# A hybrid decoder layer in one kernel: transposes ahead of the data, first loads on two queues, another bank order, the compressing preparation pinned, one multiplication moved

## The chip, the cores and the metric

The kernel runs on one core of a Trainium2 chip. The metric is the device time of one execution in microseconds (us); lower is better. TensorE (PE) multiplies, VectorE (DVE) and ScalarE (ACT) do elementwise work, GpSimd (POOL) does some elementwise work and issues stores, SyncE (SP) issues loads.

## The reference

For x of 1024 tokens by 1024 channels, in float32, one layer:

```
xn   = rmsnorm(x, norm1_w);  proj = xn @ w_in      # q, k/v of 3 branches, gates, xr, yr, 2 merge gates
A    = sparse attention(q, compressed k/v, selected blocks, window of 512), weighted by gates
B    = RG-LRU(causal conv of width 4 of xr) * gelu(yr)
x    = x + (sigmoid(g_a) * (A @ W_a_up) + sigmoid(g_b) * (B @ W_b_up)) @ W_o
out  = x + relu(rmsnorm(x) @ W1)^2 @ W2
```

The compressed keys and values are a two-layer network over blocks of 32 tokens: blocks plus a learned position, times a 2048x256 matrix, gelu, times 256x64.

## The kernel before

**Precision.** Every product of two float32 matrices is three products of 32-bit round operands: each operand is split into a high part (ACT copies it to the type fp32r) and a low part (DVE subtracts), and high*high, high*low and low*high are summed in PSUM. So each tile that TensorE takes costs ACT and DVE one operation each. For weights this is `split_w` (L197 to L202: `wh` by L200 on ACT, `wl` by L201 on DVE), with four buffers of 512 columns for each part, which is two streamed weight tiles.

**Order on the engines.** The program is written in one order, and a planner in the build gives each engine a fixed list of instructions: of those that are ready in its plan, the one that stands first in the program. An engine runs its list in order. `tc.issue_after(ins)` puts the instructions of its block that are on the engine of `ins` behind `ins` in that list.

**Stage 1, the start.** SP issues the loads: `sm` (small vectors, with the norm's scale), then for each block k of 128 channels x (`xs`, the first in two halves) and 350 columns of the attention weights (`as`). POOL builds the identity. For each k, ACT and DVE split x (`xh`, `xl`) and the weights (`ah`, `al`), and TensorE adds three products for each of six token tiles to `acc6`, six banks of PSUM: five of tag "F" and one of tag "H". Two more token tiles follow in "F" banks, and then two further thirds of the columns. Tag "H" is used again by the compressing network, tag "T" (2 banks) by transposes.

**Stage 2, eight rounds j = 0 to 7 of the RG-LRU, some 26 us each (one is longer).** The work of a round in program order: TensorE computes `fx` (xr, two halves of 512 tokens, L744 to L748), with the four gate products `pg` of round j-1 between the halves; DVE takes each half out of PSUM (L748); the convolution and its split on DVE and ACT (L666 to L676; the last of it, L676, is `lst[j]["last"]`); then the pieces of the compressing network that `PHI_AT` names for this round (one in rounds 0 to 4 and 6, two in round 5: pieces 5 and 6); then `fy` (yr, two halves, out of PSUM by L767); the end of round j-1 (L712, a scan L713 on DVE, a multiplication L714 and a store L715 on POOL); then one step of `q_proc` (L555, L556, and the rope of the tile before, L423 to L425), which is queued behind L676. `fx`, `pg` and `fy` share the five "F" banks.

A piece of the compressing network is 12 products (`Hk` or `Hv`, L602) and the preparation of the next piece, `phi_prep`: four additions on DVE (L590, `zt`), the high part on ACT (L593, `zh`) and the low part on DVE (L594, `zl`).

**After that** TensorE computes the merge gates (`fg`), the attention, the two up-projections, W_o, and the two large matrices of the feed-forward part by a scheme with seven instead of eight products of halves.

Of the kernel before, what the change touches and what calls it, by code (L numbers as in the profile page):

```python
# [10 lines left out]
F32 = mybir.dt.float32  # L11
F32R = mybir.dt.float32r
AF = mybir.ActivationFunctionType
OP = mybir.AluOpType
# [3 lines left out]
P = 128  # L18
# [7 lines left out]
AW = 350  # L26
KCOFF = 4 * S
RESERVE = 2
EARLY = 8
PAD = 32  # L30
WPRI = 200
# [31 lines left out]
def stream_order():  # L63
# [13 lines left out]
    for half in range(2):  # L77
        for c in range(8):
            yield "wo", c
    for g in range(EARLY):  # L80
        yield "f1e", g
# [11 lines left out]
def product_order(n):  # L93
    out = []
    for g in range(n):
# [3 lines left out]
        out += [(g, 7), (g, 5)]  # L99
        if g + 1 < n and g + 1 >= EARLY:  # L100
            out += [(g + 1, 1), (g + 1, 2)]
# [12 lines left out]
def gap(t, off, *dims):  # L114
    return bass.AP(tensor=t.tensor, offset=t.offset + off, ap=[t.ap[0]] + [list(d) for d in dims])
# [19 lines left out]
def layer_kernel(ctx, tc, xT, w_att, w_lru, w_nsa, w_ff2, stream, rows, small, phi_w2, consts, masks, outT, scratch=None):  # L135
    nc = tc.nc
    V, A, G, T = nc.vector, nc.scalar, nc.gpsimd, nc.tensor
# [16 lines left out]
    ident = cst.tile([P, P], F32, name="ident")  # L154
    ones2 = cst.tile([P, 2], F32, name="ones2")
    sm = cst.tile([P, NSM], F32, name="sm")
# [53 lines left out]
    def ws_get(kind):  # L210
        n = st["next"]
        assert order[n][0] == kind, (n, order[n], kind)
        st["next"] += 1
        while st["prepped"] <= n:
            ws_prep()
        return st["hl"].pop(n)
# [47 lines left out]
    psT = pools.open("psT", side="left", space=PSUM)  # L264
    psA = pools.open("psA", side="left", space=PSUM)

    def attw_load(c, k):
        raw = xs_p.tile([P, AW], F32, name=f"as{k}", tag="as") if c == 0 else wa.tile([P, AW], F32, name=f"ar{c}_{k}", tag="ar", bufs=4)
        nc.sync.dma_start(raw, w_att[c, :, k])
        return raw  # L270

    def attw_split(raw, c, k):
# [9 lines left out]
    def x_load(k):  # L282
        t = xs_p.tile([P, S], F32, name=f"xs{k}", tag="xs")
        if k == 0:
            araw[(0, k)] = attw_load(0, k)
            for hs in HS:
                nc.sync.dma_start(t[:, hs], xT[0:P, hs])
        else:
            nc.sync.dma_start(t, xT[k * P:(k + 1) * P, :])
            araw[(0, k)] = attw_load(0, k)  # L290
        xs.append(t)

    nc.sync.dma_start(sm, small)
    for k in range(NK):
        x_load(k)
    make_identity(nc, ident)
    G.memset(ones2, 1.0)
    accsq = rbc
    aw = {}
    acc6 = [psA.tile([P, 512], F32, name=f"acc{t}", tag="F" if t < 5 else "H", bufs=5 if t < 5 else 1) for t in range(6)]  # L300
    for k in range(NK):
        if k == 0:
            aw[(0, k)] = attw_split(araw.pop((0, k)), 0, k)
# [59 lines left out]
    yq = [at_p.tile([P, 512], F32, name=f"yq{t}") for t in range(NT)]  # L363
# [52 lines left out]
    def rope(pool, t, nh, cosap, sinap, name):  # L416
        tmp = pool.tile([P, nh, 16], F32, name=name, tag="rp", bufs=1)
        sw = gap(t, 8, [64, nh], [-8, 2], [1, 8])
        y = gap(t, 0, [64, nh], [8, 2], [1, 8])
        t4 = gap(tmp, 0, [16, nh], [8, 2], [1, 8])  # L420
        s4 = gap(sinap, 0, [0, nh], [8, 2], [1, 8])
        c4 = gap(cosap, 0, [0, nh], [8, 2], [1, 8])
        V.tensor_tensor(t4, sw, s4, op=OP.mult)  # L423
        V.tensor_tensor(y, y, c4, op=OP.mult)
        V.tensor_tensor(y, y, t4, op=OP.add)  # L425
# [117 lines left out]
    rowq = phi_p.tile([P, 512], F32, name="rowq")  # L543
# [8 lines left out]
    def q_proc():  # L552
        for t in range(NT):
            qq = yq[t].rearrange("p (a d) -> p a d", d=64)
            V.tensor_tensor(qq, qq, gap(facq, t * 8, [1, 8], [0, 64]), op=OP.mult)  # L555
            G.tensor_tensor(yq[t], yq[t], rowq, op=OP.mult)  # L556
            yield
            rope(phi_p, yq[t], 8, qcon[:, t * 16:t * 16 + 16], qcon[:, 128 + t * 16:144 + t * 16], f"rpq{t}")

# [22 lines left out]
    def phi_prep(which, piece):  # L582
        po = SM["pos" + which][0]
        zh = phi_p.tile([P, 4, P], F32R, name=f"zh{which}{piece}", tag="zh", bufs=2)
        zl = phi_p.tile([P, 4, P], F32R, name=f"zl{which}{piece}", tag="zl", bufs=2)
        for jp in range(2):
            for g in range(2):
                src = cn_t if jp == g else cs_t
                rs = slice(jp * 64, jp * 64 + 64)
                V.tensor_tensor(gap(zt[rs], g * 64, [P, 4], [1, 63]),  # L590
                                gap(src[rs], jp + 8 * piece, [2, 4], [16, 63]),
                                gap(sm[rs], po + piece * 4, [1, 4], [0, 63]), op=OP.add)
        A.activation(zh, zt, AF.Copy)  # L593
        V.tensor_tensor(zl, zt, zh.bitcast(F32), op=OP.subtract)  # L594
        return zh, zl

    def phi_mm(H, w, zz, piece):
        zh, zl = zz
        for jj in range(4):
            h, l = w[jj // 2]  # L600
            b = slice(jj % 2 * 256, (jj % 2 + 1) * 256)
            mm3(H[:, 0:256], zh[:, jj, :], zl[:, jj, :], h[:, b], l[:, b], piece == 0 and jj == 0, piece == 3 and jj == 3)  # L602
# [59 lines left out]
    lst = {}  # L662
# [53 lines left out]

    phi = {"H": None, "zz": None}

    def phi_piece(i):
        which, piece = ("k", i) if i < 4 else ("v", i - 4)  # L720
        if piece == 0:
            phi["H"] = psB.tile([P, 512], F32, name=f"H{which}", tag="H", bufs=1)
        phi_mm(phi["H"], ws_get("phi"), phi["zz"], piece)
        ws_done()
        if i != 3 and i < 7:
            phi["zz"] = phi_prep("k" if i < 3 else "v", (i + 1) % 4)
        if piece == 3:
            bg.append(phi_tail(which, phi["H"]))

# [2 lines left out]
    for j in range(8):  # L732
        if j == 4:
            w = ws_get("vc")
            for half in range(2):
                cjob(psB, "vc", half, w, 5)
                step()
            phi["zz"] = phi_prep("v", 0)
        w = ws_get("xr")
        xy = lt("xr", j, S + P)  # L740
        xr = xy[:, 0:S + 3]
        G.memset(xr[:, 0:3], 0.0)
        for half in range(2):
            ps = ftile(psB, f"fx{j}{half}", 5)  # L744
            fjob(ps, HS[half], w)
            if half:
                ws_done()
            V.tensor_tensor(xr[:, 3 + half * 512:515 + half * 512], ps, rbc[:, HS[half]], op=OP.mult)  # L748
            if half == 0:
                step()  # L750
                if j:
                    lru_gates(j - 1)
        lru_conv(j, xr)
        lru_one(j - 1)
        lru_split(j)
        lru_root(j - 1)
        lw_prep(j)
        step()
        for i in PHI_AT[j]:
            phi_piece(i)  # L760
        w = ws_get("yr")
        y = xr[:, 3:S + 3]
        lst[j]["y"] = y
        for half in range(2):
            ps = ftile(psB, f"fy{j}{half}", 5)
            fjob(ps, HS[half], w)
            V.tensor_tensor(y[:, HS[half]], ps, rbc[:, HS[half]], op=OP.mult)  # L767
            if half:
                ws_done()
            else:  # L770
                lru_end(j - 1)
                step()
                step()
        step()
        with tc.issue_after(lst[j]["last"].ins):
            next(q_gen, None)
# [46 lines left out]
    gmps = [psC, 1]  # L823
    left[0] -= RESERVE
    mk = ab.tile([P, NMK], F32, name="mk")
# [176 lines left out]
    for ui, u in enumerate(units):  # L1002
        n = len(blocks_of(u))
        nxt = units[ui + 1] if ui + 1 < len(units) else None
        g, i, kind = u
# [7 lines left out]
        for b in range(n):  # L1013
# [18 lines left out]
            last = b == n - 1  # L1032
# [41 lines left out]

    left[0] = RESERVE + left[0]
    ins = [(rh[k], rl[k], d_lru[k * P:(k + 1) * P, :], f"rr{k}") for k in range(8)]
# [91 lines left out]
    for half in range(2):  # L1168
        hs = HS[half]
        for c in range(8):  # L1170
# [6 lines left out]
            t = vt(f"hac{c}{half}")  # L1177
# [5 lines left out]
            if c == 0:  # L1183
                acc = sq
# [4 lines left out]
            if half and c > 1:  # L1189
                norm2(c - 2, 0)  # L1190
                if c > 3:
                    k = c - 4
# [66 lines left out]
    def ff_out(g, fh, half, t):  # L1259
        A.activation(t, t, AF.Square)  # L1260
        if (fh, half) != (0, 1):
            u_store(g, {(0, 0): "B11", (1, 0): "B21", (1, 1): "B22"}[(fh, half)], t)
        if g >= EARLY or (fh, half) != (0, 0):
            uq[(g, fh, half)] = t
# [23 lines left out]
    def ff_keep(g, name):  # L1288
        t = vt(f"{name}{g}")
        ps = ff["ps"][(g, "a")]  # L1290
        if g < EARLY and name != "P1":
            V.tensor_tensor(t, ps, ff["sv"][g]["P1"], op=OP.add)
# [13 lines left out]
    def ff_product(g, p):  # L1306
        _, bn, bank = PROD[p]
        first = p in (2, 7) or p == (6 if g < EARLY else 1)
        if first:
# [4 lines left out]
        ff_done(g, p, ps)  # L1314
        if p == 3 and g < EARLY:
            t = uq[(g, 0, 0)] = vt(f"ub{g}")
# [88 lines left out]
    for g in range(EARLY):  # L1405
# [10 lines left out]
        if g < 4:  # L1416
# [4 lines left out]
            t = vt(f"T2{g}")  # L1421
# [3 lines left out]
        else:  # L1425
            name, o, half = (("T3", 0, 1), ("T1", 0, 0), ("B22", 4, 1), ("T4", 4, 0))[g - 4]
            for k in range(4):
                t = hn[(k + o, half)]
# [14 lines left out]
    for n in range(len(steps)):  # L1443
        pi, k = steps[n]
# [27 lines left out]
        elif k == 15:  # L1472
            for d in range(4):
                for kk in range(16 - DMAJ, 16):
                    mms(kk, d)
                if p in (1, 7, 6):
                    t = rs[d]
                    V.tensor_tensor(t, ps[d], t, op=OP.add)
                    kept[(p, d)] = t
                else:  # L1480
                    t = rs[d] if p == 3 else kept.pop(({4: 6, 5: 7, 2: 1}[p], d))
                    V.tensor_tensor(t, ps[d], t, op=OP.add)
                    c, half = {2: (d, 0), 3: (d, 1), 4: (d + 4, 0), 5: (d + 4, 1)}[p]
# [81 lines left out]
```

## Time and profile before

| | |
|---|---|
| median of 3 runs | 1590.0 us (1589.86 to 1592.36) |
| the profiled execution | 1590.64 us |
| its span, first to last instruction | 1588.9 us |
| TensorE matmuls busy | 1566.3 us, 99% of the span |
| VectorE busy | 1112.0 us, 70% |
| ScalarE busy | 854.5 us, 54% |
| GpSimd busy | 290.2 us, 18% |
| mean granted TensorE clock | 0.997 |

The median is 0.64 us below the profiled execution, and the profiled execution has 1.7 us outside its span. Busy time is the share in which an engine had an instruction in flight. A time in the rows below is counted from the first instruction.

### The profile page before, as it was taken

Reading aid. Unit: us, or ns where it says so; the run is one execution under the profiler, and the core shown is the slowest. Engines: PE = TensorE matmul, PEld = TensorE weight load, DVE = VectorE, ACT = ScalarE, POOL = GpSimd, SP = SyncE. Lnnn points to the kernel's source line nnn. Section 1 sums busy time; section 2 is a strip of 40 time slices with the busy share of each in tenths; the row PEclk is TensorE's granted clock in tenths of the full one; section 3 lists DMA queues with packets and bytes.
Section 4 is the critical chain, followed back from the end, with each engine's and each line's share of the span. In section 5 each row is a group of like instructions: output and inputs, shape, how many; then the busy total and the mean of one; then the engine's idle time right before and its main releaser. Section 6 shows DMA issues by size and latency. Waiting matters only on the chain.

```text
span 1588.9 us, 21949 instructions
## 1 busy us (share of the span) xinstructions
PE 1566.3 (99%) x7541; PEld 1312.3 (83%) x7541; DVE 1112.0 (70%) x2128; ACT 854.5 (54%) x1570; POOL 290.2 (18%) x414
## 2 busy tenths in 40 slices
PE   8999999999999999999999999999999999999999
PEld 8998887887888887887788888888888888888887
DVE  8637889876888777886544447988665679665664
ACT  7435667674677566675533335744555564443432
POOL 0001222233343434432000222022211110000000
PEclk9999999999999999999999999999999999999999
DMA  6101221213011121014533544355533598553554
GB/s 228 49 22 55 93 89 58 99 74 109 31 34 41 61 64 34 31 34 155 200 114 112 180 178 159 126 204 208 184 146 146 177 390 294 164 175 138 203 199 149
DMA packets 86688, 206.80 MB, mean 130 GB/s; under 512 B 11184, under 2 KB 15792, under 8 KB 86576
## 3 DMA queue, kind: packets, MB, share of 16 engines
q1 hardware_dynamic: 71856, 157.15, 28.7%
q0 software_dynamic: 14720, 48.25, 8.3%
q8 instruction: 59, 0.97, 0.2%
q14 instruction: 53, 0.43, 0.1%
HBM read 152.93 MB, written 52.43 MB: 129 GB/s over the span
## 4 chain that ended last, share of the span: by engine, by line
PE 69%; issue 2%; ACT 2%; DVE 2%; DMA 1%; POOL 1%; ACTq 0%; DVEq 0%; POOLq 0%
PE p L1462 6%; PE p L1464 6%; PE p L1463 6%; PE pt L946 3%; PE p1a L1303 3%; PE p1a L1304 3%; PE p1a L1302 3%; PE fg L234 3%; PE fg L236 3%; PE fg L238 3%; PE p1c L1304 2%; PE po L234 2%; PE po L238 2%; PE po L236 2%; PE p1c L1303 2%
## 5 line engine op out<-in xcount | busy, mean ns | idle before, releaser
L1462 PE MATMUL p<-hu,hw 128*128 128x512 f32 x448 | 174.3, 389 | 0.0
L1463 PE MATMUL p<-lu,hw 128*128 128x512 f32 x448 | 174.3, 389 | 0.0
L1464 PE MATMUL p<-hu,lw 128*128 128x512 f32 x448 | 174.3, 389 | 0.0
L201 DVE TENSOR_TENSOR wl<-wr,wh 128x512 fp32r<-128x512 f32 x156 | 110.3, 711 | 84.8 <-ACT wh L200 79.5
L200 ACT ACTIVATE wh<-wr 128x512 fp32r<-128x512 f32 x156 | 97.3, 627 | 128.7 <-PE po L236 40.7
L951 ACT ACTIVATE ph<-pt 128x512 fp32r<-128x512 f32 x148 | 88.0, 596 | 88.0 <-PE pt L946 86.7
L1139 ACT ACTIVATE hu<-ur 128x512 fp32r<-128x512 f32 x112 | 70.0, 628 | 114.4 <-PE p L1463 108.8
L952 DVE TENSOR_TENSOR pl<-pt,ph 128x512 fp32r<-128x512 f32 x148 | 101.7, 687 | 27.7 <-ACT ph L951 25.9
L234 PE MATMUL fg<-xh,wh 128*128 128x512 f32 x256 | 112.0, 437 | 5.2 <-DVE ge L792 4.8
L1140 DVE TENSOR_TENSOR lu<-ur,hu 128x512 fp32r<-128x512 f32 x112 | 77.0, 688 | 43.3 <-ACT hu L1139 37.6
L238 PE MATMUL fg<-xh,wl 128*128 128x512 f32 x256 | 101.9, 398 | 0.0
L236 PE MATMUL fg<-xl,wh 128*128 128x512 f32 x256 | 101.5, 397 | 0.0
L1464 PEld LDWEIGHTS p<-hu,lw 128*128 128x128 f32 x448 | 84.1, 188 | 17.6
L1463 PEld LDWEIGHTS p<-lu,hw 128*128 128x128 f32 x448 | 84.1, 188 | 17.5
L1462 PEld LDWEIGHTS p<-hu,hw 128*128 128x128 f32 x448 | 84.1, 188 | 17.3
L1285 ACT ACTIVATE z<-z 128x512 f32<-128x512 f32 x56 | 35.4, 632 | 53.5 <-DVE z L1284 53.4
L201 DVE TENSOR_TENSOR wlf<-S,whf 128x512 fp32r<-128x512 f32 x64 | 42.7, 689 | 27.2 <-ACT whf L200 26.5
L234 PEld LDWEIGHTS fg<-xh,wh 128*128 128x128 f32 x256 | 48.9, 191 | 14.1 <-issue 3.5
L1257 POOL DMA_DIRECT2D d_u<-z x48 | 26.0, 542 | 186.5 <-ACT z L1260 178.7
L1139 ACT ACTIVATE hw<-wr 128x512 fp32r<-128x512 f32 x64 | 39.5, 625 | 35.9 <-DVE wr L1395 17.1
L238 PEld LDWEIGHTS fg<-xh,wl 128*128 128x128 f32 x256 | 48.6, 190 | 10.8
L974 PE MATMUL o<-ph,V 128*128 128x512 f32 x132 | 54.3, 411 | 0.0
(856 smaller groups left out, 4578.1 us busy)
## 6 DMA issues: line engine op xcount, KB each, us to landing
wr<-in_stream SPq DMA_DIRECT2D x106, 512.0 KB, 3.5
ur<-d_u SPq DMA_DIRECT2D x112, 256.0 KB, 5.3
wr<-in_w_ff SPq DMA_DIRECT2D x96, 256.0 KB, 5.3
d_u<-uT POOLq DMA_DIRECT2D x64, 256.0 KB, 3.2
d_u<-z POOLq DMA_DIRECT2D x48, 256.0 KB, 2.7
d_gm<-ge POOLq DMA_DIRECT2D x32, 256.0 KB, 2.7
g<-d_gm SPq DMA_DIRECT2D x32, 256.0 KB, 2.7
d_lru<-li POOLq DMA_DIRECT2D x8, 512.0 KB, 3.0
```

The source lines that it names most:

```text
L200: A.activation(h, src, AF.Copy)
L201: V.tensor_tensor(l, src, h.bitcast(F32), op=OP.subtract)
L234: T.matmul(ps, h[:, b], mh[k0 + k][:, sl], start=(k == 0), stop=False)
L236: T.matmul(ps, h[:, b], ml[k0 + k][:, sl], start=False, stop=False)
L238: T.matmul(ps, l[:, b], mh[k0 + k][:, sl], start=False, stop=(k == nk - 1))
L951: A.activation(ph, pst, AF.Copy)
L952: V.tensor_tensor(pl, pst, ph.bitcast(F32), op=OP.subtract)
L1139: A.activation(h, src, AF.Copy)
L1303: T.matmul(ps, h[:, b], bl, start=False, stop=False, skip_group_check=True)
L1462: T.matmul(ps[d], wh[:, b], uh, start=fresh and kk == 0, stop=False, skip_group_check=True)
L1463: T.matmul(ps[d], wh[:, b], ul, start=False, stop=False, skip_group_check=True)
L1464: T.matmul(ps[d], wl[:, b], uh, start=False, stop=kk == 15, skip_group_check=True)
```

## The change

Five edits. A scratch tile `warm` takes 14 transposes of the identity on TensorE, ahead of the first products; nothing reads it. The loads of `sm` and of the first `as` are issued by ACT, and no longer by SP. Of the six accumulators the first and no longer the last has the bank of tag "H". In `phi_piece` the preparation of the next piece is queued on DVE behind `lst[j]["last"]` (L676 of the same round). In `q_proc` the multiplication by `rowq` (L556) runs on DVE and no longer on POOL.

```
+NWARM = 14
     def attw_load(c, k):
-        nc.sync.dma_start(raw, w_att[c, :, k])
+        (nc.scalar if c == 0 and k == 0 else nc.sync).dma_start(raw, w_att[c, :, k])
...
-    nc.sync.dma_start(sm, small)
+    nc.scalar.dma_start(sm, small)
     for k in range(NK):
         x_load(k)
     make_identity(nc, ident)
+    warm = psT.tile([P, 512], F32, name="warm", tag="T", bufs=2)
+    for m in range(NWARM):
+        T.transpose(out=warm[:, m % 4 * P:(m % 4 + 1) * P], in_=ident, identity=ident)
...
-    acc6 = [psA.tile([P, 512], F32, name=f"acc{t}", tag="F" if t < 5 else "H", bufs=5 if t < 5 else 1) for t in range(6)]
+    acc6 = [psA.tile([P, 512], F32, name=f"acc{t}", tag="F" if t else "H", bufs=5 if t else 1) for t in range(6)]
...
-            G.tensor_tensor(yq[t], yq[t], rowq, op=OP.mult)
+            V.tensor_tensor(yq[t], yq[t], rowq, op=OP.mult)
...
-    def phi_piece(i):
+    def phi_piece(i, after):
...
         if i != 3 and i < 7:
-            phi["zz"] = phi_prep("k" if i < 3 else "v", (i + 1) % 4)
+            with tc.issue_after(after):
+                phi["zz"] = phi_prep("k" if i < 3 else "v", (i + 1) % 4)
...
-            phi_piece(i)
+            phi_piece(i, lst[j]["last"].ins)
```

## Rows read from the trace of the kernel before

**Rows 1.** Waits of TensorE, whole span: total us, times, longest us.

```profile
PE acc L225 <- ACT xh L305: 5.3, 1, 5.3
PE fg L234 <- DVE ge L792: 4.8, 5, 3.1
...
PE Hv L225 <- ACT wh L200: 0.3, 1, 0.3
```

**Rows 2.** Timeline of SP's first issues: start us, duration us.

```profile
0.74 0.38 SPq L293 DMA_DIRECT2D sm<-in_small  x1
1.18 0.42 SPq L269 DMA_DIRECT2D as<-in_w_att  x1
1.65 0.90 SPq L287 DMA_DIRECT2D xs<-in_xT  x2
2.59 0.43 SPq L289 DMA_DIRECT2D xs<-in_xT  x1
```

**Rows 3.** Timeline of ScalarE, second block; in brackets idle time before, and its releaser.

```profile
8.94 1.15 ACT L305 ACTIVATE xh<-xs,sm 128x1024 fp32r<-128x1024 f32 x1 [1.06 <-DMA xs<-in_xT]
```

**Rows 4.** Timeline of TensorE around the second block.

```profile
10.04 0.50 PE L225 MATMUL acc<-ah,xh 128*128 128x350 f32 x1
10.33 0.49 PE L226 MATMUL acc<-al,xh 128*128 128x350 f32 x1
...
11.89 0.43 PE L226 MATMUL acc<-al,xh 128*128 128x350 f32 x1 [0.72 <-DVE al L276]
...
12.31 0.32 PE L225 MATMUL acc<-ah,xh 128*128 128x350 f32 x1
12.47 0.33 PE L226 MATMUL acc<-al,xh 128*128 128x350 f32 x1
```

**Rows 5.** Timeline of TensorE: second half of fx in rounds 2, 3, 5, 6.

```profile
176.09 0.50 PE L234 MATMUL fx<-xh,wh 128*128 128x512 f32 x1 [0.34 <-DVE xr L748]
...
202.13 0.39 PE L234 MATMUL fx<-xh,wh 128*128 128x512 f32 x1
...
268.02 0.50 PE L234 MATMUL fx<-xh,wh 128*128 128x512 f32 x1 [2.13 <-DVE xr L748]
...
296.50 0.39 PE L234 MATMUL fx<-xh,wh 128*128 128x512 f32 x1
```

**Rows 6.** Timeline of VectorE: rope, and first half of fx out of PSUM.

```profile
171.18 1.88 DVE L423 TENSOR_TENSOR rpq<-yq,qcon 128x128 f32<-128x128 f32 x1
...
175.36 0.68 DVE L748 TENSOR_TENSOR xr<-fx,rbc 128x512 f32<-128x512 f32 x1
...
201.15 0.68 DVE L748 TENSOR_TENSOR xr<-fx,rbc 128x512 f32<-128x512 f32 x1
...
294.57 0.68 DVE L748 TENSOR_TENSOR xr<-fx,rbc 128x512 f32<-128x512 f32 x1
```

**Rows 7.** Timeline of GpSimd in the same stretch.

```profile
170.15 2.76 POOL L714 TENSOR_TENSOR li<-li,xr 128x1024 f32<-128x1024 f32 x1 [17.10 <-DVE li L713]
...
173.97 1.31 POOL L556 TENSOR_TENSOR yq<-yq,rowq 128x512 f32<-128x512 f32 x1
```

**Rows 8.** Source lines L425 and L590, VectorE: duration ns min/median/max, first and last start.

```profile
L425 DVE TENSOR_TENSOR yq<-yq,rpq x8: 272/1376/1540, 173.9 to 347.4; 128x128 f32<-128x128 f32 x8
L590 DVE TENSOR_TENSOR zt<-cn_t,sm x16: 562/580/1720, 121.3 to 270.3; 64x252 f32<-64x252 f32 x16
```

**Rows 9.** Groups of VectorE, 140 to 376 us, shapes apart: busy us, mean ns.

```profile
L555 DVE TENSOR_TENSOR yq<-yq,facq 128x512 f32<-128x512 f32 x8 | 5.4, 679 | 0.0
...
L594 DVE TENSOR_TENSOR zlv<-zt,zhv 128x512 fp32r<-128x512 f32 x4 | 2.7, 686 | 0.0
```

**Rows 10.** Timeline of ScalarE, gate products of round 1 out of PSUM.

```profile
173.75 1.37 ACT L688 ACTIVATE lr<-pg,sm 128x512 f32<-128x512 f32 x2
```

**Rows 11.** Windows (us, busy us of PE, PEld, DVE, ACT, POOL, then granted clock, DMA share, GB/s).

```profile
181.86:201.83 19.97, 19.97 (x95) 16.76 (x94) 19.82 (x22) 12.76 (x16) 4.70 (x4) 1.00 0.32 112
...
362.40:365.60 3.20, 3.18 (x8) 2.52 (x9) 0.00 (x0) 0.00 (x0) 2.80 (x3) 0.50 0.12 47
```

## The prediction

> **What bounds the kernel now.** I read the engines' shares first: TensorE is busy 99% of the span, so any change counts only by what it takes from or adds to TensorE's idle time, or by the pace of its products. The waits of TensorE then say where there is idle time to win [rows 1]: 5.3 us before the first product, 4.8 us at the merge gates, little elsewhere. The reader is to see that the largest wait is at the start, where this change has two of its five edits, and that the wait of 4.8 us is on a part that it does not touch. Next come TensorE's own rows in the rounds of stage 2 [rows 5]: the second half of `fx` follows the gate products at once in rounds 3 and 6, is 0.34 us late in round 2 and 2.13 us late in round 5, each time behind L748, which clears the bank of the first half. So VectorE is nearly the bound there: between the end of one `fx` and L748 of the next it is busy 19.82 of 19.97 us [rows 11]. The other three edits are in this stretch, so I cost the change by VectorE's work in it.
>
> **The start.** SP issues `sm`, `as` and x one after the other; x starts at 1.65, 0.91 us after the first issue [rows 2]. With two issues on ACT's queue x starts at 0.74, so all x loads may come 0.91 us earlier, or not at all if the 16 transfer engines are what is slow. What is late in the end is the second block: ScalarE gets its x at 8.94 [rows 3], and TensorE waits for the low part of its weights until 11.89 [rows 4]. Everything behind this runs without a wait of TensorE [rows 1], so it moves as a whole. I take 0.6 us, nearer to the upper bound because nothing else is in front of x. The Trainium skill speaks against more (DMA: Bandwidth & Descriptors, Issuing engines are not separate DMA queues): loads from several engines share the same transfer engines, and a second queue saves only issue time. By that rule this term is at most the issue time, 0.91 us.
>
> **The transposes.** The products of the first block follow each other every 0.29 us, those from 12.31 on every 0.16 us [rows 4]: 350 columns in 0.29 us is the pace of 1.2 GHz. If the transposes bring the faster pace forward, the 18 products of the first block take 18 x 0.13 = 2.3 us less. But TensorE had finished that block when it waited until 11.89 for the second, so I count this as nothing: it only makes that wait longer. The cover is the late second block; were it gone, the edit would be worth up to 2.3 us. The transposes need no data and lie in idle time. The Trainium skill has the rule behind it (TensorE: Matmul & The Clock Gate, Part 1): the default state is throttled and activity releases it. By that rule alone the start would come 2.3 us earlier; that is a rival below.
>
> **The banks.** The accumulator whose bank the seventh token tile takes is now the second, not the first. TensorE has no wait there in the waits view [rows 1], and "H" is next used a hundred microseconds later: 0, and no loss.
>
> **The multiplication.** On POOL it takes 1.31 us [rows 7]; on DVE the same shape takes 0.68 [rows 9]. While POOL multiplies, DVE's operations with two inputs in SBUF stand still: L423 lasts 1.88 us and ends with L714 of POOL [rows 6, 7], and L425 has a median of 1.38 us where its shortest is 0.27 [rows 8]. Without L556 L425 costs 0.27, so a round gains 1.54 - 0.27 = 1.27 us (round 1, the longest) or 1.38 - 0.27 = 1.11 (round 2, by the median) and pays 0.68. The block by L714 stays.
>
> **The pinned preparation.** One piece costs DVE four additions of 0.58 and a low part of 0.69: 3.0 us [rows 8, 9]. Before, the planner put most of them into round 0, where DVE had time, and those of pieces 6 and 7 in round 5. Behind L676 they stand in rounds 0, 1, 2 and 4 (one each) and 5 (two). The plan takes what is ready and first in the program, and the preparation stands ahead of `fy`, the scan and the rope: so I expect it right behind L676, inside the stretch that has no slack. L713, L714, the store, L767 and the rope queue behind it, and L748 behind them. Round 0 has no scan and gets rid of two pieces; rounds 3, 6 and 7 get none. For the others, how late L748 comes for the next `fx`:
>
> Round 1: 0.34 late before [rows 5], +3.0 for the piece, -0.69 for a low part that moves out, +0.68 -1.27 for the multiplication: 2.1.
> Round 2: L748 ends at 201.15 + 0.68 = 201.83 and TensorE goes on at 202.13 [rows 5, 6], a slack of 0.30; +3.0 +0.68 -1.11: 2.3 late.
> Round 4: 2.13 late before, because four additions stood ahead of L748, one blocked by POOL for 1.72 - 0.58 = 1.14 [rows 5, 8]. Others take their place, unblocked: +0.68 -1.14: 1.7 late.
> Round 5: L748 ends at 295.25, TensorE goes on at 296.50: 1.25 of slack; two pieces +6.0, +0.68, -0.69: 4.7 late.
>
> Together 10.8 us, against 0.34 + 2.13 = 2.5 before. If all of it reaches TensorE, the change costs 8.3 us here. The other bound is that none does. The second half of `fx` needs any free bank of five: ScalarE clears the first gate product at about 173.75 + 0.69 = 174.44, earlier than L748 ends (175.36 + 0.68 = 176.04) [rows 6, 10]. Before, the plan gave `fx` the bank that DVE clears; with DVE fuller in the plan, it may give ScalarE's instead, and then TensorE passes by and DVE catches up later in the round. I take half: 5.4 us, or +2.9 against before, since the trace has neither order.
>
> **Piece 6** can run only when its preparation is done, behind L676 of round 5, and no longer next to piece 5. Its weights hold half of the weight buffers until then, and its 12 products no longer cover the split of the `yr` weights, for which TensorE waited 0.3 us already [rows 1]. A bound is the length of the piece, 12 products of 256 columns at 0.16 x 256/350 = 0.12 us [rows 4], 1.4 us, the other 0; I take 0.7, or +0.4.
>
> **Sum.** -0.6 + 2.9 + 0.4 = +2.7 us on the profiled execution of 1590.64 us: 1593.3. The median lies 0.64 below: 1592.7 us.
>
> **The rivals.**
> All of it lands on TensorE. The plan keeps the bank order, since DVE's blocking by POOL, 1.6 us per round, is nowhere in its order. For it: the plan of before shows just that in rounds 2 and 5. -0.6 + 8.3 + 0.4: 1590.0 + 8.1 = 1598.1 us. Where TensorE stands still for 3 us or more, the pace falls too: after the longest wait at the merge gates, 3.1 us, the granted clock was 0.50 for 3.2 us [rows 1, 11], which costs half of that, 1.6 us, so up to 1599.7.
> None of it does: banks come from ScalarE, or the plan finds other places behind L676, and the old waits of 2.47 and 0.3 us go. -0.6 - 2.5 - 0.3: 1590.0 - 3.4 = 1586.6 us, and 1586.3 with the full 0.91. This is the other side; it decides where DVE's added 3 us per round stay clear of L748.
> The start pays in full: the second block's data come early enough that the pace of the first block counts, -2.3 on the forecast: 1590.4. Against it: the second block is late by transfer and by DVE's chain, not by products.
>
> **How the numbers follow.** This kernel's measurement tells 0.2%, or 3.2 us, from no change: below 1586.8 is faster, above 1593.2 slower. Half of the lateness (own range 1589 to 1596): 0.37, of it 0.25 within, 0.12 above. All of it: 0.25, above. None: 0.30, of it 0.20 below and 0.10 within. The start in full: 0.05, 0.04 within and 0.01 below. Another order in the attention, which no row shows: 0.03, counted as 0.02 below and 0.01 above. Faster 0.23, same 0.39, slower 0.38. The range runs from none of it with the full start, 1586.3, to all of it with one fall of the clock, 1599.7.
>
> **What would show it.** Start: ScalarE's second block before 8.94, TensorE's second block by some 11.3. Transposes: the first block every 0.16 us, then a longer wait. Multiplication: L425 at 0.27 in every round. Preparation: L590 directly behind L676, and the wait of `fx` on L748 in rounds 2, 3, 5 and 6 near 2.1, 2.3, 1.7 and 4.7 us (all), or gone (none). Piece 6: `Hv` after `fy` of round 5. The prediction is wrong if the preparation finds room that I don't see, if the banks go another way, or if a shift of the plan reaches the attention.

## The result, and the profile after

The changed kernel takes 1602.8 us, the median of 6 runs (1600.4 to 1604.2), against 1590.2 (1589.9 to 1592.4) before on the same chip: 1.0078 times the time, 95% interval 1.0068 to 1.0087. The forecast was 1592.7 with a range to 1599.7. The profiled execution took 1602.03 us with a span of 1600.3, 11.4 more than before. TensorE is busy 1569.8 us; it was 1566.3.

In the changed kernel line numbers are higher: L748 is L753, L676 is L680, L590 is L594, L594 is L598, the scan L713 is L717, L714 is L718, the rope L423 to L425 is L427 to L429, L555 and L556 are L559 and L560.

The waits of TensorE after (total us, times, longest):

```profile
PE acc L226 <- ACT ah L276: 6.7, 1, 6.7
PE fx L235 <- DVE xr L753: 5.6, 3, 2.1
PE fg L235 <- DVE ge L797: 5.3, 5, 3.5
...
PE Hv L228 <- DVE zlv L598: 3.1, 1, 3.1
```

Beside [rows 1], `fx` waits 5.6 us instead of 2.5, a wait of 3.1 us for the low part of a compressing piece is new, and the first product comes 1.4 us later. The waits in the timeline of TensorE, for [rows 5]:

```profile
178.79 0.50 PE L235 MATMUL fx<-xh,wh 128*128 128x512 f32 x1 [1.82 <-DVE xr L753]
...
207.12 0.50 PE L235 MATMUL fx<-xh,wh 128*128 128x512 f32 x1 [2.12 <-DVE xr L753]
...
274.43 0.50 PE L235 MATMUL fx<-xh,wh 128*128 128x512 f32 x1 [1.69 <-DVE xr L753]
...
294.96 0.39 PE L226 MATMUL Hv<-wh,zhv 128*128 128x256 f32 x1 [0.27 <-ACT zhv L597]
...
299.95 0.39 PE L228 MATMUL Hv<-wh,zlv 128*128 128x256 f32 x1 [3.10 <-DVE zlv L598]
```

Rounds 2, 3 and 5 wait 1.82, 2.12 and 1.69 us. What stands ahead of L753 is in VectorE's timeline of the first of these stretches, for [rows 6]:

```profile
168.41 0.58 DVE L594 TENSOR_TENSOR zt<-cn_t,sm 64x252 f32<-64x252 f32 x1
168.92 0.59 DVE L594 TENSOR_TENSOR zt<-cs_t,sm 64x252 f32<-64x252 f32 x1
...
170.14 0.58 DVE L594 TENSOR_TENSOR zt<-cs_t,sm 64x252 f32<-64x252 f32 x1
170.64 0.57 DVE L594 TENSOR_TENSOR zt<-cn_t,sm 64x252 f32<-64x252 f32 x1
171.25 2.29 DVE L717 TENSOR_TENSOR_SCAN li<-lr,lt 128x1024 f32<-128x1024 f32 x1
173.46 0.67 DVE L598 TENSOR_TENSOR zlk<-zt,zhk 128x512 fp32r<-128x512 f32 x1
174.04 0.68 DVE L772 TENSOR_TENSOR xr<-fy,rbc 128x512 f32<-128x512 f32 x1
174.64 1.88 DVE L427 TENSOR_TENSOR rpq<-yq,qcon 128x128 f32<-128x128 f32 x1
...
178.05 0.68 DVE L753 TENSOR_TENSOR xr<-fx,rbc 128x512 f32<-128x512 f32 x1
```

Four additions, the low part, and everything that was there before: in the kernel before none of these five stands between L676 (166.06) and L748 (175.36). VectorE has no gap in it, and `fx` waits for its end. The pin of round 5 works differently: the planner has moved piece 6 into the first half of `fx` of round 6, and it is the piece itself that waits there. VectorE and GpSimd, timeline:

```profile
297.07 2.83 DVE L598 TENSOR_TENSOR zlv<-zt,zhv 128x512 fp32r<-128x512 f32 x1
...
296.65 2.70 POOL L718 TENSOR_TENSOR li<-li,xr 128x1024 f32<-128x1024 f32 x1 [17.54 <-DVE li L717]
```

The low part, 0.69 us elsewhere, lasts 2.83: it stands still while GpSimd runs L718 in the same stretch, as L423 does in [rows 6, 7]. The pace of TensorE suffers too. Windows (us, busy us of PE, PEld, DVE, ACT, POOL, then granted clock, DMA share, GB/s):

```profile
208.00:210.00 2.00, 2.00 (x8) 1.59 (x7) 0.00 (x0) 1.87 (x3) 0.52 (x1) 0.66 0.00 0
210.00:212.00 2.00, 2.00 (x7) 1.54 (x6) 0.40 (x1) 1.49 (x3) 1.85 (x1) 0.50 0.04 8
212.00:214.00 2.00, 2.00 (x10) 1.64 (x9) 0.40 (x1) 1.99 (x2) 0.00 (x0) 0.98 0.00 0
...
300.00:302.00 2.00, 2.00 (x12) 1.90 (x12) 1.99 (x4) 1.47 (x2) 0.34 (x2) 0.70 0.62 246
302.00:304.00 2.00, 2.00 (x6) 1.61 (x5) 1.97 (x6) 1.95 (x4) 0.00 (x0) 0.50 0.09 25
304.00:306.00 2.00, 2.00 (x9) 1.59 (x9) 2.00 (x5) 0.60 (x1) 0.00 (x0) 0.94 0.00 0
```

Behind the waits of 2.12 and 3.10 us the granted clock falls to 0.50, the 1.2 GHz level, for some 3 to 4 us each time. The start, from the timelines of TensorE, SP, ScalarE and VectorE, for [rows 2 to 4]:

```profile
6.72 0.95 PE L226 MATMUL acc<-ah,xh 128*128 128x350 f32 x2 [6.72 <-ACT ah L276]
...
8.92 2.55 PE L300 MATMUL warm<-ident 128*128 128x128 f32 x14
11.23 0.40 PE L227 MATMUL acc<-al,xh 128*128 128x350 f32 x1
...
0.74 0.86 SPq L288 DMA_DIRECT2D xs<-in_xT  x2
...
3.94 1.28 ACT L309 ACT_TABLE_LOAD   x1 [3.94 <-DMA xs<-in_xT]
5.23 0.72 ACT L309 ACTIVATE xh<-xs,sm 128x512 fp32r<-128x512 f32 x1
6.17 0.50 ACT L276 ACTIVATE ah<-as 128x350 fp32r<-128x350 f32 x1 [0.21 <-DMA as<-in_w_att]
6.57 1.85 ACT L309 ACTIVATE xh<-xs,sm 128x512 fp32r<-128x512 f32 x2
...
4.10 0.17 DVE L467 TENSOR_SCALAR le<-sm 128x8 f32<-128x8 f32 x1 [4.10 <-DMA sm<-in_small]
```

The transposes are not ahead of the first products but among them: the planner put seven of the first block's eighteen products first. `sm` is there at 4.10 (2.55 before), the weights of the first block at 6.17 (3.79), and a table load of 1.28 us, which ran at 0.74 before, now stands behind the wait for x. x itself comes earlier: the row of 6.57 holds the second half of the first block and the second block, which ScalarE got at 8.94 before.

How much later than before TensorE reaches the same point in the two profiled executions, by the starts of the rows (the seventh token tile is the first work behind the six accumulators):

```
seventh token tile (32.08 before)     +1.22
second half of fx, round 2            +2.70   wait 1.82 instead of 0.34
second half of fx, round 3            +4.99   wait 2.12 instead of 0
products of the piece of round 3      +6.79   slow clock, 1.80
second half of fx, round 5            +6.41   wait 1.69 instead of 2.13
second half of fx, round 6           +11.79   waits of 3.37 for piece 6, slow clock for the rest
end of the span                      +11.4
```

### The profile page after: what moved, and what is told of

Read it like the earlier page. It is cut to its first block, busy times and chain, and to the rows that moved or that the text cites. A ratio compares the mean times of both kernels' runs of the same rounds, so it can differ in the third digit from the quotient of the medians.

```text
span 1600.3 us, 21976 instructions
## 1 busy us (share of the span) xinstructions
PE 1569.8 (98%) x7555; PEld 1314.2 (82%) x7555; DVE 1108.4 (69%) x2136; ACT 855.0 (53%) x1570; POOL 279.7 (17%) x406
## 4 chain that ended last, share of the span: by engine, by line
PE 68%; issue 2%; ACT 2%; DVE 2%; DMA 1%; POOL 1%; ACTq 0%; POOLq 0%; DVEq 0%
PE p L1469 6%; PE p L1468 6%; PE p L1467 6%; PE pt L951 3%; PE p1a L1307 3%; PE p1a L1308 3%; PE p1a L1309 3%; PE fg L235 3%; PE fg L239 2%; PE fg L237 2%; PE p1c L1309 2%; PE po L235 2%; PE po L239 2%; PE po L237 2%; PE p1c L1307 2%
## 5 line engine op out<-in xcount | busy, mean ns | idle before, releaser
L1467 PE MATMUL p<-hu,hw 128*128 128x512 f32 x448 | 174.3, 389 | 0.0
L1468 PE MATMUL p<-lu,hw 128*128 128x512 f32 x448 | 174.3, 389 | 0.0
L1469 PE MATMUL p<-hu,lw 128*128 128x512 f32 x448 | 174.3, 389 | 0.0
L235 PE MATMUL fx<-xh,wh 128*128 128x512 f32 x128 | 51.6, 403 | 5.6 <-DVE xr L753 5.6
```

The source lines that it names most:

```text
L235: T.matmul(ps, h[:, b], mh[k0 + k][:, sl], start=(k == 0), stop=False)
L1467: T.matmul(ps[d], wh[:, b], uh, start=fresh and kk == 0, stop=False, skip_group_check=True)
L1468: T.matmul(ps[d], wh[:, b], ul, start=False, stop=False, skip_group_check=True)
L1469: T.matmul(ps[d], wl[:, b], uh, start=False, stop=kk == 15, skip_group_check=True)
```

## The experiments

Theory A: the pinned preparation is the loss, by VectorE's lateness at L748. Rival B: the start (or another edit) is a large part of it. Each ratio is to the kernel before in runs on the same chip (medians 1589.7 to 1590.7), with its interval.

**1. The change without the pin.**

```
-            with tc.issue_after(after):
-                phi["zz"] = phi_prep("k" if i < 3 else "v", (i + 1) % 4)
+            phi["zz"] = phi_prep("k" if i < 3 else "v", (i + 1) % 4)
```

> The changed kernel without the pin of the preparation; the other four edits stay. Theory A (the pin fills VectorE's full stretches): the waits of fx on L748's counterpart in rounds 2 and 3 fall from 1.82 and 2.12 us to under 0.3, the 3.10 us wait of Hv and both falls of the clock go, and the time falls by 9 to 11 us, to 1592 to 1594. Theory B (the multiplication on VectorE fills them): those waits stay above 1.5 us and the time stays within 3 us of 1602.8. Theory C (the start costs most): within 3 us too.

1590.9 us, ratio 1.0009 (0.9999 to 1.0018). One wait of `fx` is left, 1.60 us in round 5, and none of `Hv` for its low part. By the two ratios (1.0078 and 1.0009) the pin is some 11 of the 12.6 us: theory A, with a time 1.1 below its range.

**2. The pin alone**, on the kernel before.

```
-            phi["zz"] = phi_prep("k" if i < 3 else "v", (i + 1) % 4)
+            with tc.issue_after(after):
+                phi["zz"] = phi_prep("k" if i < 3 else "v", (i + 1) % 4)
```

> The kernel before with the pin alone; the multiplication stays on GpSimd, the start as before. Theory A: waits of fx in rounds 2 and 3 of 2.4 to 3 us (0.6 and 0.4 more than in the changed kernel, as GpSimd blocks L425 again), a wait of piece 6 of about 3 us, and 9 to 13 us over 1590. Theory B: no wait over 1 us and within 2 us of 1590.

1604.0 us, ratio 1.0089 (1.0074 to 1.0104). Its waits:

```profile
PE fx L234 <- DVE xr L749: 7.5, 3, 2.7
...
PE Hv L227 <- DVE zlv L594: 3.1, 1, 3.1
```

With the block of L425 by GpSimd still there, each wait of `fx` (2.54, 2.71 and 2.28 us) is longer than in the changed kernel, and the clock fell behind each of them and behind that of `Hv`. Theory A holds, though the loss, 14.3 us, is above the 9 to 13 expected; what was left was the start.

**3. The three edits of the start alone**, on the kernel before.

```
+        (nc.scalar if c == 0 and k == 0 else nc.sync).dma_start(raw, w_att[c, :, k])
+    nc.scalar.dma_start(sm, small)
...
+        T.transpose(out=warm[:, m % 4 * P:(m % 4 + 1) * P], in_=ident, identity=ident)
...
+    acc6 = [... tag="F" if t else "H", bufs=5 if t else 1) for t in range(6)]
```

> The kernel before with the start's edits alone: transposes, two issues on ACT, bank order. Theory A: the seventh token tile starts at 33.3 us in place of 32.08, everything behind is 1.2 us late, and the time is 1591 to 1592. Rival (the start also sets off the plan of the later stages, from which most of the loss comes): 1594 or more.

1592.6 us, ratio 1.0016 (1.0006 to 1.0025). First product at 6.18, transposes from 8.64 for 2.50 us, seventh token tile at 33.04 against 32.08: a small loss, not the gain that was forecast, and 0.6 us above the range of theory A. In this execution the clock fell behind the wait of 2.12 us in round 5; in the kernel before it did not fall behind the same wait, 2.13 [rows 5].

**4. The multiplication on VectorE alone**, on the kernel before.

```
-            G.tensor_tensor(yq[t], yq[t], rowq, op=OP.mult)
+            V.tensor_tensor(yq[t], yq[t], rowq, op=OP.mult)
```

> The kernel before with the multiplication on VectorE alone. Theory A: a round of VectorE is 0.4 to 0.6 us shorter, the wait in round 2 (0.34) goes, that in round 5 (2.13) falls to about 1.7, and the time is 1589 to 1590. Theory B: waits of fx grow in every round by some 0.5 us, and the time is 1592 or more.

1588.4 us, ratio 0.9994 (0.9984 to 1.0003). L425 by duration (ns, min/median/max), for [rows 8]:

```profile
L425 DVE TENSOR_TENSOR yq<-yq,rpq x8: 277/280/293, 174.4 to 345.5; 128x128 f32<-128x128 f32 x8
```

The block is gone in every round, the wait of round 2 too, and the merge gates start 1.18 us earlier (341.51 against 342.69). The median gains about as much, but the interval includes no change.

**5. No pin, and the transposes really first**: the products of the first block are queued behind the last transpose.

```
+        wl_ = T.transpose(out=warm[:, m % 4 * P:(m % 4 + 1) * P], in_=ident, identity=ident)
...
+            with tc.issue_after(wl_.ins):          # wl_: the last transpose
                 mm3(acc6[t][:, :AW], ...)
```

> The whole change without the pin, with the products of the first block held behind the last of the fourteen transposes, so that the transposes stand wholly ahead of the first product and not among the products of the first block. Theory S1 (the transposes cost because they stand among the products, 2.5 us of them, and the data of the second block are there by about 10.2): the first block's products follow each other at 0.16 us from about 6.0 to 6.7, the seventh token tile starts at 30.4 to 31.6 against 32.83 in the run without the pin, and the time is 1588.4 to 1589.4 us, 1.5 to 2.5 below that run's 1590.88. Rival S2 (the loads set the start: whatever TensorE does ahead, it waits for the data of the second block): the seventh tile at 32.5 or later and no gain on 1590.9.

1592.0 us, ratio 1.0013 (1.0005 to 1.0022). TensorE's timeline:

```profile
1.36 3.25 PE L300 MATMUL warm<-ident 128*128 128x128 f32 x14 [1.36 <-POOL ident masks.py:199]
6.24 0.66 PE L226 MATMUL acc<-ah,xh 128*128 128x350 f32 x1 [1.62 <-ACT ah L276]
...
10.15 0.49 PE L228 MATMUL acc<-ah,xl 128*128 128x350 f32 x1
10.45 0.38 PE L226 MATMUL acc<-ah,xh 128*128 128x350 f32 x1
```

S1 failed in its first step: 3.25 us of transposes lie ahead, yet the ten products from 7.53 to 10.15 follow each other every 0.29 us, and the faster pace comes at 10.45, against 10.62 in the kernel before. The seventh tile is 1.08 us earlier than in run 1 (31.75, just outside S1's range), but more than that is given back: at 45.4 TensorE waits 1.1 us for the weights of the second column group, which wait for their load, and `fx` of round 0 starts at 119.61 against 119.09 in run 1.

**6. No pin and no transposes** (multiplication, bank and queue stay).

```
...
-        T.transpose(out=warm[:, m % 4 * P:(m % 4 + 1) * P], in_=ident, identity=ident)
```

> The whole change without the pin and without the transposes: multiplication, bank and queue stay. Theory S1: the first block runs at 0.29 us a product from about 6.0, ends near 11.3, and the seventh token tile starts at 32.0 to 32.9; the time is within 1 us of the 1590.88 of the run that has the transposes in the middle, since what they take (2.5 us) is about what the faster pace gives back (up to 2.3 us). Rival S2 (loads set the start): the first block ends early and TensorE waits for the second block's low weights or data, as it did before the change. Rival S3 (the queue is what costs): the first product at 6.0 or later, and the seventh tile later than 32.08 by as much as the first product is later than 5.29.

1588.8 us, ratio 0.9990 (0.9981 to 0.9999). First product again at 6.00, seventh tile at 32.29. The products keep the slow pace until 12.25, and still the tile is 0.54 earlier than in run 1, which has the transposes among them. S2 failed (no wait for the second block), S3 in part: the first product is 0.71 later than before, the tile only 0.21. S1 had the pace and the tile, but not the time: by the ratios this is 3 us below run 1, not within 1. Beside run 4 (0.9994), which has the multiplication without the queue and the bank order, nothing can be told. ScalarE's table load, and the load of `as` (KB, us from issue to landing; issued at 1.18):

```profile
3.54 1.28 ACT L305 ACT_TABLE_LOAD   x1 [3.54 <-DMA xs<-in_xT]
...
5.47 0.48 ACT L275 ACTIVATE ah<-as 128x350 fp32r<-128x350 f32 x1
...
as<-in_w_att ACTq DMA_DIRECT2D x1, 175.0 KB, 3.7
```

`as` is there at about 4.9, and ScalarE, late by the table load, takes it at 5.47.

**7. The whole change, pinned behind the clearing of the first half of `fx`** instead of L676.

```
-            phi_piece(i, lst[j]["last"].ins)
+            phi_piece(i, out0.ins)                 # out0: L753 of half 0, same round
```

> The change with one difference: the preparation is pinned behind the clearing of the first half of fx of the same round, not behind the last statistics operation. Theory A (the pin costs because its four additions and its low part stand between the statistics and the clearing of the next fx bank): the waits of fx for that bank are 0 in rounds 2 and 3 and below 0.3 in round 5, no wait of the phi products above 0.5, and the time is 1588.5 to 1590.5 us, 12 to 14 below the changed kernel's 1602.8. Rival (any pin of the preparation behind work of its own round costs, through the lateness of the pieces and of the weight buffers that they hold): 1595 or more.

1592.0 us, ratio 1.0010 (1.0001 to 1.0019). The loss by the pin is gone: rounds 2, 3 and 5 do not wait. One wait is left, one round on:

```profile
297.27 0.50 PE L235 MATMUL fx<-xh,wh 128*128 128x512 f32 x1 [1.68 <-DVE xr L753]
```

The additions of piece 7 are pinned in round 5 and come into the stretch before round 6; run 9, which pins them in round 6, does not have this wait. The time is 1.5 us above the range; the seventh tile is 2.04 us late, the most of all runs, with 3.19 us of transposes among the products.

**8. Transposes first, and the pin of run 7.**

```
+            with tc.issue_after(wl_.ins):
                 mm3(acc6[t][:, :AW], ...)
...
+            phi_piece(i, out0.ins)
```

> Both mended: transposes wholly ahead of the first product, preparation pinned behind the clearing of the first half of fx. Theories A and S1 together: 1586 to 1588 us, below the kernel before (1590.2) by more than 0.1%; seventh token tile at 30.4 to 31.6, no wait of fx above 0.3. Rival (the start gives nothing, or what it gives is taken up by a wait later on): 1589.5 or more.

1592.0 us, ratio 1.0010 (1.0001 to 1.0019): the rival. The faster pace came at 12.29, so 3.25 us of transposes ahead did nothing for it, and the wait at 45.7 for the next weights took 0.7 us.

**9. Only the last two pieces late**, with the multiplication: the kernel before, no edit of the start.

```
+        if i == 7:
+            with tc.issue_after(after):            # after: L748 of half 0, same round
+                phi["zz"] = phi_prep("v", 3)
         phi_mm(phi["H"], ws_get("phi"), phi["zz"], piece)
...
-        if i != 3 and i < 7:
+        if i == 5:
+            with tc.issue_after(after):
+                phi["zz"] = phi_prep("v", 2)
+        elif i != 3 and i < 6:
             phi["zz"] = phi_prep("k" if i < 3 else "v", (i + 1) % 4)
```

> The kernel before with the multiplication on VectorE, and the preparation of the last two pieces alone pinned behind the clearing of the first half of fx of the round in which the piece runs (rounds 5 and 6). Theory A (what TensorE waits for at fx is only what stands between the last statistics operation and the clearing): the one wait of fx that is left with the multiplication alone (1.61 in round 5) is gone, no wait of fx above 0.3, and the time is 1.2 to 1.8 us below that kernel's 1588.4: 1586.6 to 1587.2. Rival (a later piece makes a wait of its own, as Hv behind zlv, or the stall moves to the next round as it did when every preparation was pinned there): 1588 or more, with a wait of fx or Hv of 1 us or more.

1587.1 us, ratio 0.9981 (0.9972 to 0.9990). No wait of `fx` is left at all; the second half of round 5 starts at 264.94 against 268.02:

```profile
264.94 0.39 PE L234 MATMUL fx<-xh,wh 128*128 128x512 f32 x1
```

This is faster than both kernels, by the same mechanism that made the change slow. How much of it is the two pieces and how much the multiplication, the medians can't tell: the intervals of this run and of run 4 overlap.

**10. Run 6 with the table load ahead of x**, by an activation on a new tile of 4 bytes per partition.

```
+    tab = cst.tile([P, 1], F32, name="tab")
+    V.memset(tab, 0.0)
+    A.activation(tab, tab, AF.Exp)
     make_identity(nc, ident)
```

> The run without pin and without transposes (1588.8 us), with one activation on a zeroed tile behind ScalarE's two DMA issues, so that ScalarE's table load, 1.28 us, no longer stands behind the wait for x. Theory L (with sm on the second queue the table load has moved from 0.74, where it cost nothing, to 3.54 behind the first wait for x, and this is what delays the first product): xh of the first half starts at about 3.6 instead of 4.84, the first product at 4.8 to 5.2 instead of 6.00. Rival (sharing of the transfers: the weights of the first block land too late anyway): the first product at 5.7 or later. Time: 0 to 1.2 us below the run without it, 1587.6 to 1588.8, since the clock of the first products may take part of it back.

1612.9 us, ratio 1.0142 (1.0126 to 1.0159), which no theory had. TensorE waits no longer than before; most of its groups of matmuls are slower:

```profile
L1467 PE MATMUL p<-hu,lw 128*128 128x512 f32 x448 | 177.2, 396 | 0.0
```

396 ns where the group has 389 before (174.3 us). The first product came at 6.09, so theory L failed too.

**11. The transposes alone**, on the kernel before.

```
+    for m in range(NWARM):
+        T.transpose(out=warm[:, m % 4 * P:(m % 4 + 1) * P], in_=ident, identity=ident)
```

> The kernel before with the fourteen transposes and nothing else. They stand among the products of the first block again. Theory S3 (the transposes never bring the faster pace forward and only take TensorE's time; the cover that hides them is the wait for the second block's low weights, 0.72 us): the seventh token tile 1.2 to 2.0 us later than 32.08, time 1591.2 to 1592.2. Rival S4 (they bring the faster pace forward by as much as they take): the seventh tile at 31.8 to 32.4 and no change of the time.

1593.0 us, ratio 1.0017 (1.0008 to 1.0026). They take 2.38 us from 7.94; seventh tile +0.72, of which 0.43 is a wait for the bank of the first accumulator, and `fx` of round 0 +1.76 after a wait of 0.47 for the next weights. S3 had the sign and the place, and the median is 0.8 above its range.

**12. Run 9 with both loads on ScalarE's queue and the activation of run 10.**

```
+        (nc.scalar if c == 0 and k == 0 else nc.sync).dma_start(raw, w_att[c, :, k])
+    nc.scalar.dma_start(sm, small)
...
+    A.activation(tab, tab, AF.Exp)
```

> Multiplication on VectorE, the last two pieces' preparation pinned as in the run with these two, both early loads on ScalarE's queue with the table load ahead of x; no transposes. Theories A and L together: first product at 4.8 to 5.2, no wait of fx above 0.3, 1585.5 to 1587 us, below the kernel before by 0.2 to 0.3%. Rival (what the start wins is taken back by the clock or by the weights of the second column group): 1587 or more.

1611.7 us, ratio 1.0136 (1.0122 to 1.0151), with the new tile again, so its time tells nothing of the start. No `fx` waits in it, as theory A has it; the first product is at 5.75, so theory L failed here too.

**13. Run 10 without the new tile**: the activation works on a column of a constant tile that is there anyway.

```
+    V.memset(c1[:, 0:1], 0.0)
+    A.activation(c1[:, 0:1], c1[:, 0:1], AF.Exp)
     make_identity(nc, ident)
```

> As the run with the table load ahead of x, but the activation is done on a column of a tile that is there anyway, so that no address moves. If the shift of addresses was the cause of the 22 us: 1587.6 to 1589.4 us, the matmuls of 512 columns at a mean of 389 ns again. Of the start: theory L (the table load delays the first product): 4.8 to 5.3. Theory Q (the load of as from ScalarE's queue, which shares the transfers with x, delays it): the first product at 5.7 to 6.1, with ah waiting for the DMA of as, and no gain on the 1588.8 of the run without transposes.

1589.1 us, ratio 0.9992 (0.9983 to 1.0000). The table load is at 1.66, and the first product is still late, as theory Q has it:

```profile
3.70 0.72 ACT L307 ACTIVATE xh<-xs,sm 128x512 fp32r<-128x512 f32 x1 [0.54 <-DMA sm<-in_small]
5.20 0.49 ACT L275 ACTIVATE ah<-as 128x350 fp32r<-128x350 f32 x1 [0.79 <-DMA as<-in_w_att]
```

ScalarE is free and waits for `as`, which landed at 5.20 instead of 3.79. The seventh tile was 1.33 us earlier than before in this execution; the median shows nothing of it.

**14. A tile of 4 bytes alone**, on the kernel before.

```
     cst.tile([P, PAD], F32, name="pad")
+    cst.tile([P, 1], F32, name="pad1")
```

> The kernel before with an unused tile of one column (4 bytes per partition) behind its pad, and nothing else. Theory: all tiles behind it move by 4 bytes, and each matmul of 512 columns takes some 395 ns instead of 389: 1610 to 1614 us. Rival: the activation or the memset was the cause, and this run takes 1589 to 1592 us.

1614.1 us, ratio 1.0147 (1.0133 to 1.0160), and the same group at 177.2 us, 395 and 396 ns. Nothing else differs, so the 4 bytes, by which the tiles behind move, were the cause, and not the activation or the memset.

**15. Run 9 with only `sm` on ScalarE's queue** and the table load early, no new tile.

```
-    nc.sync.dma_start(sm, small)
+    nc.scalar.dma_start(sm, small)
...
+    A.activation(c1[:, 0:1], c1[:, 0:1], AF.Exp)
```

> The best version so far (multiplication on VectorE, the last two pieces' preparation late, 1587.1 us) with sm alone on ScalarE's queue, as on SP's ahead of x as before, and the table load early on a tile that is there. Theory Q: as lands by about 3.5 and x 0.3 to 0.4 earlier than before the change, so the first product at 4.8 to 5.1 and the time 0.2 to 0.6 below, 1586.5 to 1586.9, which this measurement can hardly tell. Rival: sm, later than x from the second queue, holds xh up, first product at 5.3 or later, and no gain.

1587.4 us, ratio 0.9978 (0.9967 to 0.9988). First product at 5.07 against 5.29, seventh tile 0.34 us earlier: the sign is that of theory Q, and the time can't be told from run 9's.

## Why the prediction was wrong

**The step that failed first: "I take half".** The lateness of L748 was worked out as 2.1, 2.3 and 1.7 us for the `fx` of rounds 2, 3 and 5, and the trace shows 1.82, 2.12 and 1.69: this part of the sum was good. The fourth, 4.7 us for round 6, did not come there; 3.37 us came at piece 6. Halving it rested on the thought that the planner might give `fx` a bank that ScalarE clears. No row showed such an order, and the plan before had waited for L748 in rounds 2 and 5 [rows 5]. All of it landed on TensorE: 9.0 us of waits instead of 2.5, so +6.5 where +2.9 and, for piece 6, +0.4 were taken. The rival that gave 1598.1 to 1599.7 had this mechanism, but the time is 3.1 us above its upper end, since it kept the gain at the start and one fall of the clock. Run 2 has waits at the same places from the pin alone, and run 7 shows that they go when the same work stands behind L748.

**The clock, the largest single miss.** The forecast itself had no fall of the clock and its rival one, 1.6 us. There were two, 1.80 us behind the wait of round 3 and about 2.0 behind that of piece 6 (5.38 us of new delay less 3.37 of waits); the granted clock in these stretches accounts for 1.7 of each. With the start's 1.22 the three terms, 1.22 + 6.5 + 3.8, make 11.5 of the 11.8 us that TensorE is late behind round 6; from there to the end it gets back 0.4, which I did not follow. Against the forecast that is 3.8 us for the clock, 3.2 for the waits and 1.8 for the start, and the clock's part hangs on the waits. I had priced it from a wait of 3.1 us [rows 1, 11] and thought of waits of 3 us or more. One of 2.12 was enough here, and in runs 2 and 9 the clock did not fall behind waits of 3.10 us, so the 3 us in my rival is no condition in either direction.

**Round 5 went another way.** I expected 4.7 us at L748. The plan moved piece 6 into the first half of `fx` of round 6, and TensorE waited for its low part, which stood behind the scan and was blocked by GpSimd. "Piece 6" was priced at 0.7 for its length; it was the place of the largest wait of the rounds. The 0.3 us that I put down to the split of the `yr` weights was a misreading: the row is a wait of `Hv` for its own weights [rows 1].

**The start had the wrong sign.** Of x the step was right: in run 6 ScalarE takes the second block at 7.56 against 8.94 [rows 3]. But x was not the only load that counts: `sm` and the first `as` had been ahead of x on one queue, and on a second queue, issued at the same times (0.74 and 1.18), they land 1.1 to 1.6 and 1.1 to 2.4 us later. The rule that I cited from the Trainium skill (DMA: Bandwidth & Descriptors, Issuing engines are not separate DMA queues) also says that DMAs from several engines interleave with each other on the same transfer engines; the trace agrees, `as` 3.79 to 5.20 in run 13. I used only its bound on the gain. The table load behind x was my first explanation, and it is half of one. In run 6 `as` was there at about 4.9 and ScalarE, behind the table load, took it at 5.47; with the table load ahead of x in run 13, `as` itself was the bound, at 5.20, and the first product came only 0.25 us earlier. The second block was ready earlier, and the first block's products and the transposes then set the time. In time the queue alone shows neither gain nor loss (run 6 beside run 4): the loss of the start is the transposes' (runs 1 and 6, run 11).

**The transposes were priced at 0 because they "lie in idle time".** I read the program's order as TensorE's. In the plan they stood among the first products, where run 11 has them at +1.76 us in the profile and about 2.5 in the median. Ahead of the products (runs 5 and 8) they were no better. The rule of the Trainium skill behind the rival (TensorE: Matmul & The Clock Gate, Part 1) says that activity releases the throttle; by it alone the transposes would bring the faster pace forward. The rows don't show it: from the first product it took 4.2 and 6.3 us with transposes ahead, and 5.3, 4.2 and 6.3 us in the kernel before and runs 4 and 6, without any. In runs 5 and 8 TensorE stood idle for 1.62 and 1.43 us between the transposes and the first product; transposes that last until the first product were not tried.

**Right:** the multiplication (L429 has a median of 0.28 us in the changed kernel, and run 4 reaches the merge gates 1.18 us earlier), and the bank order, which made no wait in any run; no run had it alone, but the 0.43 us of run 11 is a wait for the bank that it sets free. The rival "none" named the condition, the added work staying clear of L748, but not the price. Run 7 keeps every preparation clear of L748 in rounds 2, 3 and 5 and takes 1592.0 us, not 1586.6; that run 9 comes to 1587.1 is no hit, since it is another kernel, without the start's edits and with two preparations pinned instead of six.

## What to carry to other kernels

Work pinned in front of an operation that has no slack costs its length, less the work that it displaces: the sum per round was within 0.3 us wherever `fx` waited, and a discount that no row supports was an error. A wait that is added costs more than itself where the clock falls behind it, so a forecast that adds waits should carry that term in the sum and not only in a rival. Before a preparation is moved, ask which instruction of that engine TensorE waits for next, and put it right behind that one. A small load gains nothing from a queue of its own if it thereby loses its place ahead of the large ones, and instructions that are meant to fill idle time must be tied there, since a planner that knows only the program's order need not put them there.

## What the runs showed of the hardware

A shift of all later tiles by 4 bytes per partition makes the kernel 22 to 24 us slower (runs 10 and 14; run 13 without the shift is back). In most groups a matmul of 512 columns takes 395 to 396 ns instead of 389; `pg` and `pb`, among others, keep their 389 to 391. The Trainium skill speaks of SBUF lines of 16 bytes and a penalty for each access that crosses to a new one (SBUF — State Buffer, Door 1: The DMA port swizzle). Whether that is what slows these matmuls no run here shows, and which operand's tile pays was not separated.

The clock behind a wait differs between executions. In the rounds of stage 2 it did not fall behind waits of 1.82 us or less, did fall behind every one of 2.28 or more (run 2 and the changed kernel), and of the waits of 2.1 us it fell behind two (the changed kernel's in round 3, run 3's) and not behind two (the one of [rows 5], run 11's). Behind the merge gates' wait of 3.06 to 3.54 us the products stay at half the pace for 2.8 us (run 5) to 6.2 us (run 1), and in runs 2 and 9, with waits of 3.10 us, the clock did not fall at all. Run 9 (the window in the order of [rows 11]):

```profile
359.74 0.47 PE L234 MATMUL fg<-xh,wh 128*128 128x512 f32 x1 [3.10 <-DVE ge L799]
...
359.70:361.70 2.00, 1.96 (x9) 1.65 (x10) 0.00 (x0) 0.00 (x0) 2.00 (x2) 1.00 0.00 0
```

So single profiles differ by up to 3.1 us there with nothing changed in that part, and the length of a wait alone does not tell whether the clock falls. Differences of 1 us between two profiles were not read as effects here unless their rows showed where they arose.
